# Conditioning vectors of two adaLN layers: one layer in pairs of chunks on TensorE, the other summed on VectorE, and a token-major mLSTM output

## The chip, the cores and the metric

One core of one Trainium2 chip. The metric is the device time of one execution in microseconds (us), smaller is better. Engines: PE (TensorE), DVE (VectorE), ACT (ScalarE), POOL (GpSimd), SP (the queue that issues nearly all loads).

## The reference, cut to what matters

```python
def hybrid_layer(xl, xc, c, c_ctx, w_ada, b_ada, ...):
    mod_l = (jax.nn.silu(c) @ w_ada + b_ada)[:, None, :]
    mod_c = jax.nn.silu(c_ctx) @ w_ada + b_ada
    sh1_l, sc1_l, g1_l, sh2_l, sc2_l, g2_l = jnp.split(mod_l, 6, -1)
    ...
    hl = rms_norm(xl, norm_mix) * (1.0 + sc1_l) + sh1_l
    hc = rms_norm(xc, norm_mix) * (1.0 + sc1_c) + sh1_c
    ...                      # attention, bidirectional mLSTM, pooling
    xl = xl + g1_l * (jnp.concatenate([att_l, ml_l, pool_l], -1) @ w_out)
    h2l = rms_norm(xl, norm_ffn) * (1.0 + sc2_l) + sh2_l
    xl = xl + g2_l * swiglu(h2l, w_ffn_gate, w_ffn_up, w_ffn_down)
    ...                      # the same for the context xc, in layer 0 alone
```

All in float32: model width 1024, 256 latent and 256 context tokens, two such layers, then a second block of another kind that the change does not touch. `w_ada` is 1024 x 6144 per layer (24 MB): six parts of 1024 columns (0 `sh1`, 1 `sc1`, 2 `g1`, 3 `sh2`, 4 `sc2`, 5 `g2`), multiplied with two vectors, `c` and `c_ctx`. Layer 1 leaves the context's output out, so of its parts 2 to 5 only the vector `c` is needed.

## The kernel before, in words

**Order of the work.** Layer 0: prologue (normalization, first three projections), mixer (17 projections of `w_in`, mLSTM, attention, pooling), `w_out` with the next norm ("norm0"), a FFN in two halves of 11 tiles, "norm1". Layer 1: the same for the 256 latent tokens, then the second block. Inside the mixer, generators of projections, mLSTM, attention, pooling, `w_out` and conditioning are drawn in turn by `_mix` with the numbers of the table `MIX` (line 24); a scheduler then sets the order on each engine.

**Weights.** Every dense product runs as three products of split operands (`mm3`, lines 234 to 238). `weights` (line 223) loads a tile of 512 KB into a ring of four (`wr`, by SP, line 220), ACT copies it to `wh` (line 229) and DVE makes the rest `wl` (line 230); `wh` has three buffers, `wl` two. A load into a slot of `wr` waits until what was in the slot has been read.

**Conditioning** (`ada`, lines 364 to 395). A layer's 6144 columns are 24 chunks of 256. Per chunk: two tiles of 512 KB into the same ring `wr`, eight matmuls in which the vectors, padded to 32 columns (`cs`), are stationary and the weights move (line 375; four groups of 32 PSUM rows hold partial sums over k), an ACT copy to `ade` (line 384), two transpositions (line 387), and on DVE a sum over the four groups, the bias and for two of the parts a third operation (lines 389 to 393). Layer 0 takes 8 chunks in the prologue and 16 in its mixer; layer 1 takes 10 in the mixer of layer 0, 2 each in norm0 and norm1, and 10 in its own mixer.

```python
            for k0 in (0, 4):
                _, v = self.raw(w, k0, 4, 256 * ch, 256)
                for g in range(4):
                    nc.tensor.matmul(bank[32 * g:32 * g + 32, 0:256], self.cs[:, k0 + g, :], v[:, g, :],
                                     start=k0 == 0, stop=k0 == 4)
```

**FFN of layer 0.** `ffn_up` (gate, silu, up, product at line 733, split at line 258) and `resid` (down) draw one dense product after another. No conditioning runs here before the change.

**mLSTM.** `hs` holds the outputs as [token, head, tile, 64]; at the end it is scaled by its inverse norm, and each pair of heads of a tile is gathered to `hc` by DVE (line 967) and transposed (line 968). The stabilizer M goes to DRAM (`Md`) through SP.

Of the kernel before, what the change touches and what calls it, by code (L numbers as in the profile page):

```python
# [23 lines left out]
MIX = {0: {'order': 'k0 g q0 v1 v0 a2 k1 q1 av a1 a0 a3 ak o0 p0 o1 p1', 'ada_own': 16, 'ada_next': 10, 'proj': 2, 'ml': 5, 'att': 1, 'fill': 1, 'late': 3, 'ada': 1, 'split': 0, 'split2': 1}, 1: {'order': 'ak k0 g a0 v0 q0 a1 av k1 q1 v1 a2 a3 p0 o0 o1 p1', 'ada_own': 10, 'ada_next': 0, 'proj': 3, 'ml': 9, 'att': 2, 'fill': 1, 'late': 1, 'ada': 1}, 2: {'in': 4, 'att': 2, 'solve': 1, 'att2': 5, 'gate': 1, 'even': 1, 'odd': 1, 'fill': 9, 'early': 5}, 'ada_ffn': [0, 0], 'norm0': 2, 'norm1': 2}  # L24
# [128 lines left out]
def _run(g):  # L153
    for _ in g:
        pass


class Builder:
    def __init__(self, tc, ctx, a):
# [10 lines left out]
        self.reg, self.reg_ins, self.reg_use = None, None, []  # L170
        self.rooms = []
# [42 lines left out]
    def raw(self, w, k0, nk, c0, cw, t=None):  # L214
# [5 lines left out]
        self.last = self.nc.sync.dma_start(v, ap).ins.name  # L220
# [130 lines left out]
    def norm_first(self, x, rr, segs, xh, xl):  # L351

        nc = self.nc
        for k in range(8):
            xr, t = (self.wk.tile([128, self.wt], F32, name=n) for n in ("sq", "nt"))
            (nc.gpsimd if k % 3 == 2 else nc.vector).tensor_mul(xr, x[:, k], rr)
            for s, e, A, B in segs:
                nc.scalar.activation(xh[:, k, s:e], xr[:, s:e], AF.Identity, bias=B(k), scale=A(k))
                nc.vector.tensor_scalar(t[:, s:e], xr[:, s:e], A(k), B(k), op0=OP.mult, op1=OP.add)
            nc.vector.tensor_sub(xl[:, k], t, xh[:, k].bitcast(F32))  # L360
            yield


    def ada(self, l, n, ahead=0, at=(3,)):
# [5 lines left out]
        def products(i, ch):  # L370
            bank = self.ps(at[i % len(at)], [128, 512])
            for k0 in (0, 4):
                _, v = self.raw(w, k0, 4, 256 * ch, 256)
                for g in range(4):
                    nc.tensor.matmul(bank[32 * g:32 * g + 32, 0:256], self.cs[:, k0 + g, :], v[:, g, :],  # L375
                                     start=k0 == 0, stop=k0 == 4)
            return bank

        banks = []
        for i, ch in enumerate(todo):  # L380
            banks += [products(j, todo[j]) for j in range(len(banks), min(n, i + ahead + 1))]
# [4 lines left out]
            for i in range(2):  # L386
                nc.tensor.transpose(pt[:, i, :], e[:, 128 * i:128 * i + 128], self.ident)
            m = mod[:, 2 * ch:2 * ch + 2, :]
            nc.vector.tensor_reduce(m, pt.rearrange("p n (g j) -> p n j g", g=4)[:, :, 0:2, :], axis=AX.X, op=OP.add)
            nc.vector.tensor_add(m, m, vec[f"b_ada{l}"][:, 2 * ch:2 * ch + 2, None].to_broadcast([128, 2, 2]))  # L390
            if ch // 4 in (1, 4):
                nm, k = vec[f"norm_mix{l}" if ch // 4 == 1 else f"norm_ffn{l}"], 2 * (ch % 4)
                nc.vector.scalar_tensor_tensor(m, m, 1.0, nm[:, k:k + 2, None].to_broadcast([128, 2, 2]),
# [4 lines left out]
    def first(self):  # L398
        nc, a, tc = self.nc, self.a, self.tc
        x = self.x = self.xp.tile([128, 8, 512], F32, name="x")  # L400
        with ExitStack() as es:
# [11 lines left out]

            add, _, r = self.squares(512)
# [11 lines left out]
            self.ada_todo = [[4, 0, 5, 1, 6, 2, 7, 3] + list(range(8, 24)) for _ in range(2)]  # L426
            pre = self.layer(0, r, self.ada(0, 8, 1, (1,)), None)
# [12 lines left out]
    def layer(self, l, pre, beside, done):  # L440
# [8 lines left out]
        with ExitStack() as es:  # L449
            ap = es.enter_context(tc.tile_pool(name=f"mix{l}", bufs=1, reuse_waits="tile"))  # L450
            if both:
                xh, xl = self.normed()
                norm = self.norm_first(x, pre, [(0, 256, m(1, 1), m(0, 1)), (256, 512, m(1, 0), m(0, 0))], xh, xl)
# [1200 lines left out]
```

## Time and profile before

| | |
|---|---|
| median of 3 runs | 1876.68 us (1875.64 to 1877.19) |
| the profiled execution, its own time | 1877.25 us |
| its span in the profile | 1875.5 us |
| PE busy | 1805.5 us, 96% |
| DVE / ACT / POOL busy | 59% / 49% / 14% |
| bytes moved | 279.32 MB, mean 149 GB/s |

"Busy" is the share of the span in which the engine executes. A chain that ended last names at each step what released it. Windows give, for a stretch of the span, the busy time of each engine (and its count of instruction records), the granted clock of PE as a share of 2.4 GHz, the share of the DMA engines in use, and what they moved. One matmul of `ada` leaves two records.

The stages that the change touches, by their bounds in the span: prologue 0 to 58 us, layer 0's mixer 58 to 300 (projections until about 193.6, then attention, mLSTM and pooling), norm0 300 to 340, layer 0's FFN 340 to 700, norm1 700 to 735, layer 1's mixer 735 to 890.

### The profile page before, as it was taken

To read this page: it belongs to the slowest core of one execution; us is meant where nothing else is said; L and a number is where in the kernel's file an instruction comes from. 1 tells how busy PE (TensorE), PEld (TensorE's weight loads), DVE (VectorE), ACT (ScalarE), POOL (GpSimd) and SP (SyncE) were. 2 spreads that over 40 slices of the span, in tenths; PEclk is the share of its full clock that TensorE was granted. 3 is DMA by queue.
4 is the path that set the end of the run, shared out by engine and by line. 5 is a ranking of instruction groups with operands and counts; after the bars stand their busy time and mean duration, and the time that the engine had idled before them with its cause. 6 is when DMAs were issued, how large, how long until landed. Compare 5 with 4: busy or idle time off the path is not lost.

```text
span 1875.5 us, 34091 instructions
## 1 busy us (share of the span) xinstructions
PE 1805.5 (96%) x13552; PEld 1593.1 (85%) x13552; DVE 1112.7 (59%) x2122; ACT 918.4 (49%) x1654; POOL 261.6 (14%) x357
## 2 busy tenths in 40 slices
PE   7999999999999999999999999998999999899998
PEld 4677567888888897877999999998999988799998
DVE  4566656433333365786676655667878864466654
ACT  4455467322222365656554644446676544454443
POOL 1011423000000021231000210012565010010000
PEclk8999999999999999999999999999999999999999
DMA  9443567432333265345666656666554540166664
GB/s 295 131 129 91 180 202 234 126 91 77 103 104 99 75 180 169 111 141 178 183 185 197 191 171 182 182 194 169 158 140 124 136 128 11 39 177 179 184 184 127
DMA packets 490608, 279.32 MB, mean 149 GB/s; under 512 B 18241, under 2 KB 487241, under 8 KB 490321
## 3 DMA queue, kind: packets, MB, share of 16 engines
q1 hardware_dynamic: 490016, 275.33, 50.5%
q8 instruction: 106, 1.74, 0.4%
q10 hardware_dynamic: 432, 1.82, 0.3%
q14 instruction: 54, 0.43, 0.1%
HBM read 274.99 MB, written 2.12 MB: 148 GB/s over the span
## 4 chain that ended last, share of the span: by engine, by line
PE 83%; DVE 5%; DMA 5%; ACT 3%; issue 3%; POOL 1%; SPq 0%; ACTq 0%; POOLq 0%; DVEq 0%
PE pd L236 17%; PE pd L238 17%; PE pd L237 17%; PE p L236 6%; PE p L237 6%; PE p L238 6%; PE p L375 2%; DMA wr<-in_w_in_dram 1%; DVE wl L230 1%; DMA wr<-in_w_ada_dram 1%; PE p L808 1%; PE p L789 1%; PE p L1498 1%; ACT wh L229 1%; PE p L940 1%
## 5 line engine op out<-in xcount | busy, mean ns | idle before, releaser
L229 ACT ACTIVATE wh<-wr 128x1024 fp32r<-128x1024 f32 (+4 forms) x450 | 436.6, 972 | 628.5 <-PE pd L237 311.1
L230 DVE TENSOR_TENSOR wl<-wr,wh 128x1024 fp32r<-128x1024 f32 (+4 forms) x450 | 509.7, 1134 | 176.8 <-PE pd L238 98.7
L236 PE MATMUL pd<-xh,wh 128*128 128x256 f32 (+1 forms) x1168 | 362.8, 312 | 13.5 <-ACT wh L229 7.4
L238 PE MATMUL pd<-xh,wl 128*128 128x256 f32 (+1 forms) x1168 | 358.0, 307 | 1.5 <-DVE wl L230 1.3
L236 PEld LDWEIGHTS pd<-xh,wh 128*128 128x128 f32 x1168 | 224.6, 193 | 31.1 <-ACT wh L229 9.1
L238 PEld LDWEIGHTS pd<-xh,wl 128*128 128x128 f32 x1168 | 224.9, 193 | 15.7 <-DVE wl L230 5.6
L236 PE MATMUL pd<-hh,wh 128*128 128x256 f32 (+1 forms) x781 | 228.3, 294 | 0.0
L237 PE MATMUL pd<-hl,wh 128*128 128x256 f32 (+1 forms) x781 | 227.4, 293 | 0.0
L237 PE MATMUL pd<-xh,wh 128*128 128x256 f32 x792 | 225.8, 285 | 0.0
L238 PE MATMUL pd<-hh,wl 128*128 128x256 f32 (+1 forms) x781 | 223.5, 294 | 0.2 <-DVE wl L230 0.2
L315 POOL TENSOR_TENSOR ssa<-ssa,sq 128x256 f32<-128x256 f32 x54 | 49.4, 915 | 796.2 <-ACT sq L313 525.6
L237 PEld LDWEIGHTS pd<-xh,wh 128*128 128x128 f32 x792 | 152.3, 192 | 1.6 <-issue 1.2
L236 PEld LDWEIGHTS pd<-hh,wh 128*128 128x128 f32 x781 | 146.8, 188 | 4.8
L237 PEld LDWEIGHTS pd<-hl,wh 128*128 128x128 f32 x781 | 146.7, 188 | 4.6
L238 PEld LDWEIGHTS pd<-hh,wl 128*128 128x128 f32 x781 | 144.8, 188 | 4.9 <-DVE wl L230 0.4
L237 PE MATMUL pd<-xl,wh 128*128 128x512 f32 (+1 forms) x376 | 132.4, 354 | 0.0
L733 DVE TENSOR_TENSOR sg<-sg,p 128x256 f32<-128x256 f32 (+1 forms) x66 | 33.6, 510 | 158.4 <-PE p L238 158.1
L236 PE MATMUL p<-xh,wh 128*128 128x256 f32 (+1 forms) x360 | 103.1, 286 | 0.0
L238 PE MATMUL p<-xh,wl 128*128 128x256 f32 x352 | 99.8, 283 | 0.0
L237 PE MATMUL p<-xh,wh 128*128 128x256 f32 x352 | 99.8, 283 | 0.0
L237 PEld LDWEIGHTS pd<-xl,wh 128*128 128x128 f32 x376 | 72.9, 194 | 11.2 <-issue 1.5
L687 DVE SCALAR_TENSOR_TENSOR x<-pd,mod,x 128x256 f32<-128x256 f32 x88 | 40.9, 480 | 67.2 <-PE pd L238 67.2
(471 smaller groups left out, 3871.8 us busy)
## 6 DMA issues: line engine op xcount, KB each, us to landing
wr<-in_w_ada_dram SPq DMA_DIRECT2D x96, 512.0 KB, 4.4
wr<-in_w_in_dram SPq DMA_DIRECT2D x92, 512.0 KB, 3.8
wr<-in_w_ffn_gate_dram SPq DMA_DIRECT2D x44, 512.0 KB, 3.7
wr<-in_w_ffn_up_dram SPq DMA_DIRECT2D x44, 512.0 KB, 3.8
wr<-in_ffn_w_gate_dram SPq DMA_DIRECT2D x44, 512.0 KB, 3.8
wr<-in_ffn_w_up_dram SPq DMA_DIRECT2D x44, 512.0 KB, 3.8
wr<-in_ffn_w_down_dram SPq DMA_DIRECT2D x32, 448.0 KB, 3.7
wr<-in_w_out_dram SPq DMA_DIRECT2D x40, 256.0 KB, 3.1
```

The lines of the kernel that those rows point to most:

```text
L229: nc.scalar.activation(h[:, :n], t[:, :n], AF.Copy)
L230: nc.vector.tensor_sub(l[:, :n], t[:, :n], h[:, :n].bitcast(F32))
L236: mm(ps, wh, xh, start=start, stop=False)
L237: mm(ps, wh, xl, start=False, stop=False)
L238: mm(ps, wl, xh, start=False, stop=stop)
L315: eng.tensor_add(acc, acc, sq)
L375: nc.tensor.matmul(bank[32 * g:32 * g + 32, 0:256], self.cs[:, k0 + g, :], v[:, g, :], start=k0 == 0, stop=k0 == 4)
L687: nc.vector.scalar_tensor_tensor(x[:, n, s:s + 256], ps[:, s - c0:s - c0 + 256], g(n), x[:, n, s:s + 256], op0=OP.mult, op1=OP.add)
L733: nc.vector.tensor_mul(g, g, ps)
L789: nc.tensor.matmul(s, qq[:, e, 128 * qt:128 * qt + 128], kk[:, kv, i, 0:128 * nk], start=i == 0, stop=i == 1)
L808: nc.tensor.matmul(po[64 * e:64 * e + 64, :], avt[:, kt, 64 * kv:64 * kv + 64], pts[e][:, kt, :], start=kt == 0, stop=kt == nk - 1)
L940: nc.tensor.matmul(po[:, t - lo, :], wt[d][s][t], mvt[:, s, h, :], start=i == 0, stop=i == len(use) - 1)
```

## The change

Four parts.

1. `ada` serves layer 0 but for part 5, and the last two pairs of layer 1, in **pairs** of chunks: 16 matmuls into one bank, one ACT copy, two transpositions, two DVE additions (a third operation for some parts). A pair loads four tiles of 512 KB. Four pairs stand in the prologue (with a ring `wa` of seven tiles of their own), six in layer 0's mixer (in the ring `wr`), one each in norm0 and norm1 (layer 1, chunks 20 to 23, part 5).
2. `ada_sums`, new: part 5 of layer 0 and parts 0 to 4 of layer 1, in twelve halves of 512 columns, **on DVE during layer 0's FFN**. A half takes eight tiles of 128 x 512 (256 KB, a ring `ar` of four, by SP), each multiplied by the vector's element and accumulated (`av`); for six halves with both vectors, for six with `c` alone. PE then sums over the partitions with a stationary `sums` of 32 columns (8 or 4 matmuls of 128 columns), ACT copies, PE transposes once, DVE adds the bias. Two steps are drawn after each dense product of the FFN.
3. In the prologue x times its inverse norm is computed before the conditioning (`xr`), and `gate` keeps the SP loads of further `w_in` weights behind the last conditioning load.
4. In the mLSTM `hs` becomes [token, tile, head, 64], is scaled head by head, and the transpositions read it directly; the 12 copies `hc` are gone. `Md` is written by ACT's queue.

```diff
-MIX = {0: {..., 'ada_own': 16, 'ada_next': 10, ...}, 1: {..., 'ada_own': 10, 'ada_next': 0, ...}, ..., 'ada_ffn': [0, 0], 'norm0': 2, 'norm1': 2}
+MIX = {0: {..., 'ada_own': 6, ...}, 1: {...}, ..., 'norm0': 1, 'norm1': 1}
...
-        self.last = self.nc.sync.dma_start(v, ap).ins.name
+        d = self.nc.sync.dma_start(v, ap).ins
+        if self.gate:
+            self.tc.add_manual_dep(d, self.gate, NOSYNC, reason="what comes first goes first")
+        self.last = d.name
...
-        def products(i, ch):
+        def products(i, c, step):
             bank = self.ps(at[i % len(at)], [128, 512])
...
+            for k0 in range(0, 8, 4):
+                if step == 1:
+                    ts = [self.raw(w, k0 + k, 2, 256 * c, 512, new_raw())[1] for k in (0, 2)]
+                    v = lambda k, j: ts[k // 2][:, k % 2, 256 * j:256 * j + 256]
+                else:
+                    ts = [self.raw(w, k0, 4, 256 * (c + j), 256, new_raw())[1] for j in (0, step)]
+                    v = lambda k, j: ts[j][:, k, :]
+                for k in range(4):
+                    for j in range(2):
+                        g = 2 * (k % 2) + j
+                        nc.tensor.matmul(bank[32 * g:32 * g + 32, 0:256], self.cs[:, k0 + k, :], v(k, j),
+                                         start=k0 + k < 2, stop=k0 + k > 5)
...
+            nc.vector.tensor_add(m, pv[:, 0, :, :, 0:2], two(wide(vec[f"b_ada{l}"])))
+            nc.vector.tensor_add(m, m, pv[:, 1, :, :, 0:2])
...
+    def ada_sums(self, todo):
+        steps = [(t, k) for t in todo for k in range(8)]
...
+                t = self.sgp.tile([128, 512], F32, name="ar", bufs=4)
+                nc.sync.dma_start(t, self.a["w_ada"][l][128 * k:128 * k + 128, 1024 * p + 512 * h:1024 * p + 512 * h + 512])
...
+        for i, ((l, p, h, js), k) in enumerate(steps):
+            load(i + 3)
...
+            for j, v in zip(js, vs):
+                c = self.cs[:, k, j:j + 1]
+                if k:
+                    nc.vector.scalar_tensor_tensor(v, t, c, v, op0=OP.mult, op1=OP.add)
+                else:
+                    nc.vector.tensor_scalar(v, t, c, None, op0=OP.mult)
+            if k < 7:
+                yield
+                continue
+            bank = self.ps(1, [128, 256])
+            for j, v in enumerate(vs):
+                for g in range(4):
+                    nc.tensor.matmul(bank[32 * g:32 * g + 32, 0:128], self.sums[:, j], v[:, 128 * g:128 * g + 128],
+                                     start=j == 0, stop=j == n - 1)
+            e = self.wk.tile([128, 256], F32, name="ade")[:, 0:128]
+            nc.scalar.activation(e, bank[:, 0:128], AF.Copy)
+            nc.tensor.transpose(bank[:, 128:256], e, self.ident)
...
-            self.ada_todo = [[4, 0, 5, 1, 6, 2, 7, 3] + list(range(8, 24)) for _ in range(2)]
-            pre = self.layer(0, r, self.ada(0, 8, 1, (1,)), None)
+            self.ada_todo = [(k, 4) for k in range(4)] + [(c, 1) for c in range(8, 20, 2)], [(20, 1), (22, 1)]
+            xr = self.room("xr", [128, 8, 512])
+            for k in range(8):
+                (nc.gpsimd if k % 3 == 2 else nc.vector).tensor_mul(xr[:, k], x[:, k], r)
+            pre = self.layer(0, xr, self.ada(0, 4, 1, (1,), self.ring("wa", [128, 1024], 7)), None)
...
+                    if k == 6:
+                        self.gate = self.last
...
-                ada = _chain(self.ada(l, n["ada_own"], at=(2,)), self.ada(1, n["ada_next"], at=(2,)))
+                ada = self.ada(l, n["ada_own"], at=(2,)) if both else iter(())
...
-                _run(_mix((up, 4), (self.ada(1, MIX["ada_ffn"][f] if both else 0, 1, (1,)), 1)))
+                if both and f == 0:
+                    ahead = self.ada_sums([(0, 5, h, (0, 1)) for h in range(2)] +
+                                          [(1, p, h, (0, 1)) for p in (1, 0) for h in range(2)] +
+                                          [(1, p, h, (0,)) for p in (2, 4, 3) for h in range(2)])
+                _run(_until(up, 1, (ahead, 2)) if both else up)
...
-            nc.sync.dma_start(self.Md[d, :, 0:T], M[32 * d:32 * d + 4, T0:])
+            nc.scalar.dma_start(self.Md[d, :, 0:T], M[32 * d:32 * d + 4, T0:])
...
-        hs = ap.tile([128, 4, ntt, 64], F32, name="hs")
+        hs = ap.tile([128, ntt, 4, 64], F32, name="hs")
...
-                hc = ap.tile([128, 2, 64], F32, name="hc", bufs=1)
-                nc.vector.tensor_copy(hc, hs[:, 2 * tl:2 * tl + 2, t, :])
-                nc.tensor.transpose(ps[:, t, :], hc.rearrange("p a b -> p (a b)"), self.ident)
+                nc.tensor.transpose(ps[:, t, :], hs[:, t, 2 * tl:2 * tl + 2, :].rearrange("p a b -> p (a b)"), self.ident)
```

How the order on the engines moves, at three places.

PE, in layer 0's mixer between projections, before: one chunk (line 375) with its transpositions (line 387) among the mLSTM's products (lines 908 and 940) and the last matmul of a projection.

```order
L238 MATMUL pd<-xh,wl 128x512
L375 MATMUL p_1186<-wr,cs 32x256 x8
L908 MATMUL p_1174<-qs,ks 128x256 x2
L908 MATMUL p_1300<-qs,ks 128x256 x2
L513 MATMUL p_1288<-sq,cm 128x512
L387 MATMUL p_1186<-cm,ade 128x128 x2
```

The same kind of place in the changed kernel (its line 387 is the matmul of `ada`, 399 the transposition, 1000 and 1032 the mLSTM's products, 240 to 242 those of `mm3`).

```order
L1032 MATMUL p_776<-mvt,W_767 128x65
L387 MATMUL p_794<-wr,cs 32x256 x16
L1000 MATMUL p_931<-qs,ks 128x512 x2
L1000 MATMUL p_945<-qs,ks 128x512 x2
L240 MATMUL pd<-xh,wh 128x512
L241 MATMUL pd<-xl,wh 128x512
L399 MATMUL p_794<-cm,ade 128x128 x2
```

A pair's 16 matmuls stand together, after the 5th, 7th, 9th, 11th, 13th and 15th of the 17 projections, and the next projection follows with little between.

PE, late in layer 0's mixer, in the attention's scores, transpositions and products (lines 789, 802, 808), before: a chunk every second step.

```order
L375 MATMUL p_2156<-wr,cs 32x256 x8
L789 MATMUL p_2453<-kk,qq 128x256 x2
L802 MATMUL p_2358<-cm,pr 128x128 x4
L789 MATMUL p_2488<-kk,qq 128x256 x2
L387 MATMUL p_2156<-cm,ade 128x128 x2
L808 MATMUL p_2238<-pt,avt 64x256 x7
L802 MATMUL p_2430<-cm,pr 128x128 x2
L375 MATMUL p_2189<-wr,cs 32x256 x8
```

There in the changed kernel (lines 881, 894, 900).

```order
L894 MATMUL p_2268<-cm,pr 128x128 x4
L881 MATMUL p_2324<-kk,qq 128x256 x2
L894 MATMUL p_2285<-cm,pr 128x128 x4
L900 MATMUL p_2240<-pt,avt 64x256
L881 MATMUL p_2338<-kk,qq 128x256 x2
L894 MATMUL p_2301<-cm,pr 128x128 x4
```

The attention's steps follow one another with no conditioning between them.

DVE, in layer 0's FFN, before: the split of weights (line 230), the product of gate and up (733) and its split (258).

```order
L733 TENSOR_TENSOR sg<-sg,p_3563 128x512
L230 TENSOR_TENSOR wl<-wr,wh 128x1024
L258 TENSOR_TENSOR hl<-sg,hh 128x512
L230 TENSOR_TENSOR wl<-wr,wh 128x1024
```

There in the changed kernel (825, 234 and 262 are those three lines, 441 and 443 the accumulation of `ada_sums`).

```order
L825 TENSOR_TENSOR sg<-sg,p_3244 128x512
L234 TENSOR_TENSOR wl<-wr,wh 128x1024
L262 TENSOR_TENSOR hl<-sg,hh 128x512
L443 TENSOR_SCALAR av_3334<-ar,cs 128x512
L443 TENSOR_SCALAR av_3335<-ar,cs 128x512
L441 SCALAR_TENSOR_TENSOR av_3334<-ar,cs,av_3334 128x512
L441 SCALAR_TENSOR_TENSOR av_3335<-ar,cs,av_3335 128x512
L234 TENSOR_TENSOR wl<-wr,wh 128x1024
```

Four accumulations stand between two weight splits, one split per dense product. On PE the sums over partitions come as 72 matmuls in 18 separate places among the FFN's products.

## Rows read from the trace of the kernel before

**Rows 1.** The page: busy time by engine, and the chain that ended last.

```profile
PE 1805.5 (96%) x13552; PEld 1593.1 (85%) x13552; DVE 1112.7 (59%) x2122; ACT 918.4 (49%) x1654; POOL 261.6 (14%) x357
...
PE 83%; DVE 5%; DMA 5%; ACT 3%; issue 3%; POOL 1%; SPq 0%; ACTq 0%; POOLq 0%; DVEq 0%
```

**Rows 2.** Windows by stage: bounds, length, busy per engine, clock, DMA share, GB/s.

```profile
0.00:58.00 58.00, 45.68 (x258) 26.84 (x258) 28.29 (x72) 24.16 (x43) 5.93 (x9) 0.88 0.84 267
58.00:193.60 135.60, 126.82 (x700) 99.32 (x700) 84.44 (x202) 67.49 (x140) 16.99 (x17) 0.97 0.37 109
193.60:300.00 106.40, 99.83 (x759) 61.11 (x752) 60.18 (x204) 61.26 (x152) 32.16 (x50) 1.00 0.69 218
340.00:700.00 360.00, 358.99 (x1764) 298.87 (x1763) 132.94 (x172) 114.49 (x163) 8.98 (x12) 1.00 0.35 102
735.00:890.00 155.00, 149.13 (x1071) 122.12 (x1069) 115.11 (x293) 96.80 (x207) 36.48 (x43) 0.98 0.48 141
```

**Rows 3.** The same windows, line 375 alone (PE, PEld).

```profile
58.00:193.60 135.60, 6.79 (x96) 2.61 (x96) 0.97 0.37 109
193.60:300.00 106.40, 23.09 (x328) 8.47 (x320) 1.00 0.69 218
735.00:890.00 155.00, 10.95 (x144) 4.05 (x144) 0.98 0.48 141
```

**Rows 4.** The same windows, line 387 alone (the transpositions).

```profile
193.60:300.00 106.40, 8.17 (x42) 5.20 (x42) 1.00 0.69 218
```

**Rows 5.** Prologue: PE's timeline (start, length, what), last conditioning product.

```profile
46.76 1.07 PE L375 MATMUL p<-wr,cs 128*32 128x256 f32 x16
```

**Rows 6.** Prologue: a window between loads.

```profile
30.00:35.00 5.00, 5.00 (x40) 2.79 (x39) 0.50 (x3) 0.47 (x2) 0.00 (x0) 1.00 0.49 161
```

**Rows 7.** PE's timeline around one chunk in a dense stretch.

```profile
169.97 0.40 PE L237 MATMUL pd<-xl,wh 128*128 128x512 f32 x1
170.20 0.39 PE L238 MATMUL pd<-xh,wl 128*128 128x512 f32 x1
170.52 1.07 PE L375 MATMUL p<-wr,cs 128*32 128x256 f32 x16
171.52 0.50 PE L236 MATMUL pd<-xh,wh 128*128 128x512 f32 x1
171.86 0.39 PE L237 MATMUL pd<-xl,wh 128*128 128x512 f32 x1
```

**Rows 8.** SP's timeline, two stretches of weight loads.

```profile
171.22 0.99 SPq L220 DMA_DIRECT2D wr<-in_w_in_dram  x2
...
294.19 15.58 SPq L220 DMA_DIRECT2D wr<-in_w_out_dram  x13
```

**Rows 9.** The page, DMA issues: count, KB each, us to landing.

```profile
wr<-in_w_in_dram SPq DMA_DIRECT2D x92, 512.0 KB, 3.8
```

**Rows 10.** ACT's timeline: the copy of those weights and its wait.

```profile
176.36 1.06 ACT L229 ACTIVATE wh<-wr 128x1024 fp32r<-128x1024 f32 x1 [2.54 <-DMA wr<-in_w_in_dram]
```

**Rows 11.** Windows in layer 0's mixer (columns as in rows 2).

```profile
150.00:160.00 10.00, 8.37 (x33) 7.31 (x34) 8.11 (x19) 5.86 (x11) 0.00 (x0) 0.66 0.63 193
170.00:180.00 10.00, 7.33 (x56) 5.57 (x54) 5.63 (x14) 4.18 (x8) 3.11 (x5) 1.00 0.41 110
266.69:282.88 16.19, 15.63 (x137) 9.29 (x136) 8.98 (x40) 12.14 (x34) 4.69 (x8) 1.00 0.82 265
```

**Rows 12.** ACT's groups by form in 266.69 to 282.88.

```profile
L384 ACT ACTIVATE ade<-p 128x256 f32<-128x256 f32 x4 | 1.5, 386 | 2.0 <-PE p L375 1.9
```

**Rows 13.** DVE's groups by form, whole span: count, busy us, mean ns.

```profile
L230 DVE TENSOR_TENSOR wl<-wr,wh 128x1024 fp32r<-128x1024 f32 x308 | 380.5, 1236 | 123.6 <-PE pd L238 79.7 <-issue 21.0 <-ACT wh L229 16.7
...
L733 DVE TENSOR_TENSOR sg<-sg,p 128x512 f32<-128x512 f32 x22 | 15.1, 687 | 102.0 <-PE p L238 102.0
...
L731 DVE SCALAR_TENSOR_TENSOR sg<-sg,sb 128x256 f32<-128x256 f32 x22 | 10.5, 478 | 0.0
...
L263 DVE SCALAR_TENSOR_TENSOR raw<-x,mod,raw 128x256 fp32r<-128x256 f32 x8 | 5.4, 672 | 0.1
```

More of the change, by code (lines that the diff above doesn't have):

```diff
@@ L170, in __init__ @@
         self.reg, self.reg_ins, self.reg_use = None, None, []
+        self.gate = None
         self.rooms = []
@@ L368, in ada @@
         todo = [self.ada_todo[l].pop(0) for _ in range(n)]
-        def products(i, ch):
+        def products(i, c, step):
             bank = self.ps(at[i % len(at)], [128, 512])
[L372 to L376, printed above, removed]
+            new_raw = lambda: new() if new else None
+            for k0 in range(0, 8, 4):
[10 more added lines that the diff above has]
+                                         start=k0 + k < 2, stop=k0 + k > 5)
             return bank
         banks = []
-        for i, ch in enumerate(todo):
-            banks += [products(j, todo[j]) for j in range(len(banks), min(n, i + ahead + 1))]
+        for i, (c, step) in enumerate(todo):
+            banks += [products(j, *todo[j]) for j in range(len(banks), min(n, i + ahead + 1))]
             bank = banks[i]
@@ L385, in ada @@
             pt = bank[:, 256:512].rearrange("p (i q) -> p i q", i=2)
[L386 to L393, printed above, removed]
+            for j in range(2):
+                nc.tensor.transpose(pt[:, j, :], e[:, 128 * j:128 * j + 128], self.ident)
@@ L412, in first @@
                 self.fn(cs[:, :, j], vec[n], AF.Silu)
+            self.sums = cst.tile([128, 2, 32], F32, name="sums")
+            nc.gpsimd.memset(self.sums, 0.0)
+            for j in range(2):
+                nc.gpsimd.memset(self.sums[:, j, j:j + 1], 1.0)
             add, _, r = self.squares(512)
@@ L573, in layer @@
                 for k in range(0, 8, 2):
-                    next(beside)
-                    if k < 6:
+                    if k:
                         next(beside)
+                    if k == 6:
+                        self.gate = self.last
                     if k:
@@ L581, in layer @@
                 products(6)
-                for _ in range(2):
+                for _ in range(4):
                     self.close_room()
@@ L595, in projections @@
                         self.late_consts()
+                        self.gate = None
             if both:
@@ L663, in layer @@
                     self.columns2()
-                _run(self.resid(rows, hs, ks, T0, 512, m(5, 1), m(5, 0), None if both else done))
+                res = self.resid(rows, hs, ks, T0, 512, m(5, 1), m(5, 0), None if both else done)
+                _run(_until(res, 1, (ahead, 2)) if both else res)
     def normed(self):
```

61 lines of the change are left out of this document (48 added, 13 removed).

## Prediction, written before the changed kernel ran

> **What bounds the kernel now.** I read the busy times and the chain first [rows 1]: TensorE is busy for 96% of the span and makes 83% of the chain, no other engine reaches 60%. So time is saved only where PE executes less or waits less, and lost where work is laid on PE or another engine is pushed past PE's pace. Next the windows by stage [rows 2]. What matters there is length minus PE's busy time: the projections of layer 0 (58 to 193.6 us) hold 8.8 us of waits, the rest of that mixer (193.6 to 300) 6.6, layer 1's mixer 5.9, layer 0's FFN only 1.0. DVE has 227 us free of 360 in that FFN, and the DMA moves 102 GB/s there against 218 in the attention. The change moves work from places where everything is busy to the place with the most room; the question is what PE pays for it.
>
> **Price of a chunk.** Conditioning alone [rows 3] shows 16 records per chunk: 6 chunks among the projections, 20.5 in the rest of the mixer, 9 in layer 1's. In the dense stretch [rows 7] matmuls start 0.23 us apart. From 170.20 to 171.86 two such spacings (0.46) should pass, and 1.66 do: the chunk costs 1.20, namely 1.00 of its own and 0.09 going in and 0.11 coming out. A transposition is 8.17/42 = 0.195 us [rows 4]. A chunk is 1.20 + 0.39 = 1.59 us of PE; a pair, with one switch and two transpositions, 2.00 + 0.20 + 0.39 = 2.59.
>
> **The change, part by part.**
>
> *Prologue: -5 us (-2 to -10).* The bytes are the same: 8 chunks. Their loads no longer stop: from 30 to 35 us the DMA was at half share and 161 GB/s [rows 6], against 267 over the prologue [rows 2], because each chunk waited for a slot of the ring; the own ring of seven and the `gate` keep conditioning in front. The last conditioning product, at 46.76 [rows 5], could come some 9 us earlier, but then normalization and first products must follow; I take half. Upper bound -10 (all of it), lower -2 (norm and `w_in` behind the gate are late instead). One copy less per pair and x*r ahead of time lie beside the loads: nothing.
>
> *Projections of layer 0: +15 (+8 to +25).* Six pairs cost 15.5 against 9.5 for six chunks: +6. Then the wait. A pair takes all four slots of `wr`, so the next two projections' weights start loading only when its matmuls have begun: for one chunk, that began at 170.52, the loads were issued 0.70 later [rows 7, 8]; landing takes 3.8 us in the median [rows 9] (here ACT began 5.14 after the issue [rows 10]), the copy 1.06. So the next projection starts about 0.7 + 3.9 + 1.06 + 0.2 = 5.9 us after the pair, and PE has its 2.2 and some 0.7 of mLSTM products meanwhile: 3.0 of wait for five pairs, half of that for the last, 16.6 in all. The 8.8 of waits before are of the same kind and go: +8. Bounds: landing at 3.8 with twice the cover gives half of it, 5.14 in place of 3.9 adds 7. For the clock +1: 0.66 in 150 to 160 (full and half speed mixed, two thirds of the time at 1.2 GHz), where PE is idle for 1.6 of 10 us, but 1.00 in 170 to 180 with 2.7 idle [rows 11]. So waits of this size do not by themselves bring half speed.
>
> *Rest of layer 0's mixer: -27 (-19 to -34).* 20.5 chunks leave PE, 20.5 x 1.59 = 32.6 us. Not all comes back: in an eight-step stretch of attention (16.19 us) PE is busy 15.63, of which four chunks are 6.4, and ACT 12.14, of which the four copies `ade` are 1.5 [rows 11, 12]. Without them ACT needs 10.6 and PE 9.3: ACT and its chain with DVE become the bound, and I take 12.5 to 14 per eight steps, not 10.6. On the other hand the last chunks hold up the loads of `w_out` on SP, which stream only from 294.19 [rows 8]; those are now loaded ahead: some 6 us of waits. -34 is chunks and waits without loss, -19 attention at 14.5.
>
> *norm0 and norm1: -1.* One pair for two chunks, 2.59 for 3.18, twice.
>
> *FFN of layer 0: +11 (+8 to +15).* The new PE work stands in the open, since PE is full here [rows 2]. 72 matmuls of 128 columns: eight of 256 took 1.00 [rows 7], so by columns 72 x 0.0625 = 4.5, by count 9.0; 5 taken, as they are of the same four groups. 18 places with 0.20 of switching: 3.6. Twelve transpositions: 2.3. ACT's twelve copies and the additions are hidden. On DVE a half with two vectors adds 16 operations of 128 x 512 to 4 splits (1.236), 2 products (0.687) and 2 splits of 128 x 512 (taken the same) [rows 13]. Of the form used there is only a 128 x 256, 0.478; from 512 to 1024 columns an operation grows by 0.549, so 256 more give 0.478 + 0.27 = 0.75 us (bounds: 0.687, a plain product of that size, and 2 x 0.672, the slowest row of that form). That makes 12.0 + 7.7 = 19.7 us in the 96 matmuls of four projections, 22.1: 89%, it fits. A half with `c` alone needs 13.7. The extra 25 MB raise the DMA here from 102 to about 172 GB/s, well under what it moves elsewhere [rows 2]. SP's loads of `ar` wait for DVE, and weights queue behind them, but the weights run four tiles ahead.
>
> Here the Trainium skill speaks against the change: TensorEngine Tiling (Array Packing), section Tiling Modes (Key Properties), says that changing the tiling mode drains TensorE, and sums with 32 stationary columns change it twice at each place. The trace agrees, 0.09 and 0.11 us [rows 7]; without it the FFN's term would be 7.3, with it 10.9.
>
> *Layer 1's mixer: -13 (-7 to -17).* Ten chunks of 1.59 = 15.9 leave it. PE waits more there once it is lighter (ACT is busy 96.8 and DVE 115 of 155 [rows 2]); 3 given back, at worst half.
>
> *mLSTM.* Twelve small copies on DVE before the transpositions, and a queue for `Md`, at the mixers' ends: within the two mixers' terms, nothing of its own (0 to -1).
>
> The sum: -5 + 15 - 27 - 1 + 11 - 13 = -20, from the profiled 1877.25 to 1857.2; the median of the runs lies 0.57 below it, so **1857 us**.
>
> **Rivals.**
>
> *A: the clock pays for the pairs.* Each of the six waits after a pair costs a stretch like that of 150 to 160: 10 us at 0.66, 3.4 us each [rows 11], 20 in place of 1. Then 1876, no change. For it: a pair's wait is longer than a chunk's. Against it: 170 to 180, at full clock with more idle time; and the whole of 58 to 193.6 has 0.97 [rows 2], which is 4 us lost over all its waits. Chance 0.12. The Trainium skill, TensorE: Matmul & The Clock Gate (HAM oscillation), describes just this: waits for DMA between short stretches of products send the array back to half speed. One window here agrees (0.66), another with more idle time does not (1.00).
>
> *B: slower; DVE becomes the bound in the FFN.* With 16 accumulations in 22.1 us less 7.7, it decides at 0.90 us each. At 1.2 the half takes 4.8 us too long, at 1.34 (twice 0.672 [rows 13]) 7.1; six halves with two vectors make 28 to 42, so 1885 to 1899. For it: the slow rows of that form, and an accumulation that reads its own last result. Against it: the 0.478 row, and POOL's 9 us in 360, while it is busier elsewhere [rows 2]. Chance 0.10.
>
> *C: better.* The waits after pairs are filled (the order leaves mLSTM and attention beside them): +5 in place of +15; attention runs at the pace of ACT's busy time, -34; layer 1 gives back nothing, -17. Then 1836. For it: PE follows at once wherever data is there (FFN: 1.0 us of waits). Against it: attention's chain runs through four engines, and weights after a pair cannot have been loaded. Chance 0.16.
>
> That the change does not do what it says is out: the order shows the pairs, the sums and an attention without conditioning.
>
> **How the numbers follow.** The forecast has 0.62, with a range of its own of 1844 to 1870: the terms' half-ranges of 4, 8.5, 7.5, 3.5 and 5, added as independent ones, make 13. A, B and C have 0.12, 0.10 and 0.16. About 0.2%, 3.8 us, is what a measurement of this kernel can tell from no change. Faster: forecast, C and a little of A, 0.80; same: most of A, 0.08; slower: B and the upper edge of A, 0.12. The range 1836 to 1879 leaves out B, half of C and the upper edge of A: 0.2.
>
> **What would show it.** Prologue: no conditioning product after some 40 us. Projections: six waits of about 3 us of `pd` for `wh`, each behind a pair, and the stretch about 15 longer. Attention: eight steps in 12.5 to 14 us, waits for ACT. FFN: about 371 us, DVE near 60% over it and near 90% in its first half, accumulations of 0.75 us. Layer 1's mixer about 142. The forecast is wrong if the accumulations exceed 0.9 us, if the clock falls below 0.9 over the projections, or if the attention does not quicken.

## The result, and the profile after

The change makes the kernel slower: 1904.39 us median of 5 runs (1900.22 to 1908.63) against 1875.64 for the kernel before in the same job, ratio 1.0151, 95% interval 1.0135 to 1.0167. The prediction was 1857 us, with a range of 1836 to 1879. The profiled execution is the slowest of the five runs, 1908.63, with a span of 1906.8, so the stages below differ by 31.3 us in sum where the medians differ by 28.75.

The page of the changed kernel, answering to [rows 1] (busy time by engine, then the chain):

```profile
PE 1806.2 (95%) x13252; PEld 1593.5 (84%) x13252; DVE 1192.3 (63%) x2200; ACT 908.7 (48%) x1630; POOL 262.5 (14%) x366
...
PE 84%; DVE 5%; ACT 3%; DMA 3%; issue 2%; POOL 1%; SPq 0%; POOLq 0%; ACTq 0%; DVEq 0%
```

PE is as busy as before, 1806.2 us against 1805.5, although conditioning takes less of it. To see where the time lies, both executions are cut at the same pieces of work: the last product of the first three projections, the last copy of a projection of layer 0, the first FFN product of layer 0, its last gate or up product, the first FFN product of layer 1. Before (bounds, length, busy time by engine, clock, DMA share, GB/s):

```profile
0.00:57.10 57.10, 45.26 (x257) 26.79 (x257) 27.73 (x71) 23.26 (x41) 5.93 (x9) 0.88 0.85 271
57.10:194.50 137.40, 128.14 (x706) 99.96 (x705) 85.19 (x203) 68.78 (x143) 17.65 (x17) 0.98 0.37 108
194.50:330.80 136.30, 128.13 (x990) 86.41 (x987) 84.45 (x256) 86.15 (x209) 45.53 (x65) 0.99 0.70 219
330.80:643.50 312.70, 311.59 (x1370) 253.16 (x1370) 105.87 (x133) 87.50 (x114) 1.70 (x2) 0.99 0.32 95
643.50:889.50 246.00, 236.18 (x1749) 202.56 (x1748) 167.72 (x381) 147.66 (x299) 50.86 (x63) 0.98 0.52 152
```

And after:

```profile
0.00:57.70 57.70, 47.05 (x249) 27.59 (x249) 27.02 (x63) 21.63 (x37) 5.89 (x12) 0.85 0.85 268
57.70:246.00 188.30, 156.63 (x828) 115.64 (x826) 91.86 (x227) 74.25 (x155) 20.52 (x22) 0.86 0.37 114
246.00:361.70 115.70, 100.16 (x600) 73.78 (x598) 66.84 (x182) 74.18 (x177) 41.23 (x63) 0.94 0.24 72
361.70:686.60 324.90, 323.79 (x1525) 256.07 (x1526) 199.41 (x293) 90.38 (x126) 1.70 (x2) 0.99 0.54 169
686.60:922.60 236.00, 223.45 (x1568) 197.70 (x1568) 164.59 (x357) 142.78 (x288) 51.69 (x66) 0.96 0.41 114
```

| stage | before | after | difference | forecast |
|---|---|---|---|---|
| prologue | 57.1 | 57.7 | +0.6 | -5 |
| projections of layer 0 | 137.4 | 188.3 | **+50.9** | +15 |
| rest of that mixer, norm0 | 136.3 | 115.7 | -20.6 | -27.5 |
| FFN of layer 0, most of it | 312.7 | 324.9 | +12.2 | +11 |
| norm1 and layer 1's mixer | 246.0 | 236.0 | -10.0 | -13.5 |
| all behind | 986.0 | 984.2 | -1.8 | 0 |

(norm0 and norm1 were forecast together at -1; half of it is put to each.) Four of five terms came out within 7 us. The projections alone are 36 us beyond theirs, and that is more than the whole gain hoped for.

**What the 50.9 us are.** PE's idle time there went from 9.3 us (137.4 - 128.14) to 31.7, so 22.4 is waiting. The other 28.5 is busy time, and the pairs explain 6 of it. The granted clock fell from 0.98 to 0.86: in the trace 51.0 us of this stretch lie at half clock (1.2 GHz) and PE is busy in 43.4 of them, against 6.8 before. Work at half clock takes nearly twice as long, as the spacing of matmuls below shows, so the clock cost at most half of the difference, some 18 us. What is left, some 4 us, is work that has moved into the stretch: by the counts of matmuls, 24 of the attention, the pooling and the end of the mLSTM lie in it now that lay behind it before. The waits, by what ended them (PE in 57.7 to 246; total us, times, longest):

```profile
PE pd L240 <- ACT wh L233: 13.4, 9, 3.4
PE p L387 <- ACT nd L1035: 6.3, 4, 2.7
PE p L399 <- ACT ade L396: 4.5, 3, 3.0
```

The first is the wait for weights that the forecast had. The other two it did not have: a pair's first matmul waits until ACT has read the mLSTM's output from the same PSUM bank, and its transpositions wait for the copy `ade`, with little or nothing else between them.

One pair, on PE's timeline (start, length, what, in brackets the idle time before):

```profile
224.76 1.93 PE L387 MATMUL p<-wr,cs 128*32 128x256 f32 x32
227.19 0.44 PE L399 MATMUL p<-cm,ade 128*128 128x128 f32 x2 [0.50 <-ACT ade L396]
231.02 0.79 PE L240 MATMUL pd<-xh,wh 128*128 128x512 f32 x1 [3.39 <-ACT wh L233]
...
234.18 0.63 PE L240 MATMUL pd<-xh,wh 128*128 128x512 f32 x1
234.60 0.63 PE L241 MATMUL pd<-xl,wh 128*128 128x512 f32 x1
235.03 0.63 PE L242 MATMUL pd<-xh,wl 128*128 128x512 f32 x1
...
236.22 0.39 PE L242 MATMUL pd<-xh,wl 128*128 128x512 f32 x1
236.45 0.39 PE L240 MATMUL pd<-xh,wh 128*128 128x512 f32 x1
236.68 0.39 PE L241 MATMUL pd<-xl,wh 128*128 128x512 f32 x1
```

From the pair's start to the next projection 6.3 us pass, and over the six pairs 5.9 to 9.0; the forecast worked out 5.9. What it missed stands behind the wait: matmuls follow one another at 0.42 us, until near 236, and only then at the 0.23 of [rows 7]. That is half clock, and it follows every pair: in the trace's record of the clock it begins 4.5 to 9.2 us after the start of each of the six. Three windows of 8 us show one turn of it; 0.58 is mostly 1.2 GHz, and 1.00 is 2.4:

```profile
170.00:178.00 8.00, 5.53 (x15) 4.18 (x14) 4.99 (x10) 2.94 (x4) 0.00 (x0) 0.58 0.73 247
178.00:186.00 8.00, 8.00 (x35) 6.48 (x35) 0.00 (x0) 1.18 (x2) 0.00 (x0) 1.00 0.00 1
186.00:194.00 8.00, 7.79 (x58) 6.92 (x56) 5.24 (x18) 4.90 (x11) 2.48 (x2) 1.00 0.00 0
```

The DMA column shows where the wait for weights comes from. It runs at 247 GB/s, then stands still for 16 us, and then all is wanted at once. SP's queue has the same turn:

```profile
195.52 0.99 SPq L221 DMA_DIRECT2D wr<-in_w_in_dram  x2
196.61 10.03 SPq L221 DMA_DIRECT2D wr<-in_w_ada_dram  x4
225.46 1.72 SPq L221 DMA_DIRECT2D wr<-in_w_in_dram  x2
```

The weights of two projections, four tiles of conditioning, and then nothing until 225.46, because all four slots of the ring hold tiles for a pair that PE reaches at 224.76.

### The profile page after: what moved, and what is told of

The parts are those of the page before. It is cut to its first block, busy times and chain, and to the rows that moved or that the text cites. A ratio compares the mean times of both kernels' runs of the same rounds, so it can differ in the third digit from the quotient of the medians.

```text
span 1906.8 us, 33662 instructions
## 1 busy us (share of the span) xinstructions
PE 1806.2 (95%) x13252; PEld 1593.5 (84%) x13252; DVE 1192.3 (63%) x2200; ACT 908.7 (48%) x1630; POOL 262.5 (14%) x366
## 4 chain that ended last, share of the span: by engine, by line
PE 84%; DVE 5%; ACT 3%; DMA 3%; issue 2%; POOL 1%; SPq 0%; POOLq 0%; ACTq 0%; DVEq 0%
PE pd L240 18%; PE pd L242 18%; PE pd L241 18%; PE p L242 6%; PE p L240 6%; PE p L241 6%; DMA wr<-in_w_in_dram 2%; PE p L900 1%; PE p L1032 1%; PE p L387 1%; DVE wl L234 1%; PE p L1588 1%; PE p L894 1%; ACT wh L233 1%; PE p L881 1%
## 5 line engine op out<-in xcount | busy, mean ns | idle before, releaser
L241 PE MATMUL pd<-xl,wh 128*128 128x512 f32 (+1 forms) x376 | 137.3, 367 | 0.0
L441 DVE SCALAR_TENSOR_TENSOR av<-ar,cs,av 128x512 f32<-128x512 f32 x126 | 89.8, 747 | 10.2 <-DMA ar<-in_w_ada_dram 9.4
```

Source lines behind the costliest of these rows:

```text
L241: mm(ps, wh, xl, start=False, stop=False)
L441: nc.vector.scalar_tensor_tensor(v, t, c, v, op0=OP.mult, op1=OP.add)
```

## The experiments

All are the changed kernel with one edit, unless another is named. Ratios are to the kernel before, run on the same chip.

### The pairs without their loads

The matmuls stay and multiply a constant. The conditioning of parts 2 to 4 of layer 0 is not computed.

```diff
             for k0 in range(0, 8, 4):
-                if step == 1:
+                if still:
+                    v = lambda k, j: self.cm[:, 0:256]
+                elif step == 1:
...
-                ada = self.ada(l, n["ada_own"], at=(2,)) if both else iter(())
+                ada = self.ada(l, n["ada_own"], at=(2,), still=True) if both else iter(())
```

> The changed kernel, but the six pairs of layer 0's mixer multiply a constant that already lies in SBUF instead of weights: their 24 loads of 512 KB are left out (so the conditioning of parts 2 to 4 of layer 0 is not computed), their 96 matmuls, copies and transpositions stay. Theory (ring): a pair's four tiles fill the whole ring of weights, the next projection's weights load only afterwards, PE idles and its clock falls; without the loads the projections (57.9 to 246 us, 188 us) fall to about 143 to 148, PE's idle time there from 31.7 to some 8 to 10, the granted clock from 0.86 to 0.96 or more, the whole to 1860 to 1866 us. Rival 1 (pairs themselves): the 32-column matmuls, the transposition's wait for the copy and the bank shared with the mLSTM cause it; then only the 13.4 us of waits for weights go, the clock stays under 0.9 and the whole is 1888 to 1892. Rival 2 (order): the mLSTM's new order causes it; then nothing changes, 1902 to 1906.

Measured: 1867.30 us, ratio 0.9948 (0.9926 to 0.9970). The projections take 139.0 us, idle time is 6.9 and the clock 0.91. Cut at 158 us:

```profile
55.90:158.00 102.10, 101.58 (x556) 78.87 (x555) 62.38 (x124) 53.39 (x103) 16.36 (x15) 1.00 0.31 83
158.00:194.90 36.90, 30.52 (x176) 23.79 (x176) 23.58 (x74) 15.21 (x41) 4.16 (x4) 0.68 0.03 8
```

Up to 158 us, with three of the pairs in it, PE idles for 0.5 us and the clock is full. So 32-column matmuls do not by themselves bring the clock down, and with the loads 49 of the 50.9 us are gone: both rivals, at 1888 us or more for the whole, are out. One thing is not separated. Without the loads the scheduler also set the pairs further apart, after some 7, 11 and 14 of the 17 projections and two more at 16, so the waits for the bank and for the copy may have gone with the distance. Three details differ from what was expected. The stretch fell below 143, partly because one pair now stands after the projections; the clock is 0.91 instead of 0.96, all of it lost in the last 37 us, where PE idles for 6.4 us again, on the mLSTM (3.1 for `qs`) and once on the bank at a pair (2.1); and the whole is 1.3 us above the 1866 expected.

### PE kept busy in the waits

```diff
+            if busy:
+                d = self.ps(1, [128, 512])
+                for _ in range(busy):
+                    f = nc.tensor.matmul(d[:, :384], self.ident, self.cm[:, :384], start=True, stop=True)
+                    self.tc.add_manual_dep(f.ins, m.ins.name, NOSYNC, reason="behind the pair")
             return bank
...
-                ada = self.ada(l, n["ada_own"], at=(2,)) if both else iter(())
+                ada = self.ada(l, n["ada_own"], at=(2,), busy=6) if both else iter(())
```

> The changed kernel with six matmuls of 128 x 384 on a constant added behind each of the mixer's six pairs; their result is not used. They do nothing but keep PE occupied while it waits for weights. At full clock they take 3.8 us per pair, about what a pair's wait for weights takes, 23 us in all if none of it lay in the waits. Theory (clock): the projections lose as much by half clock as by idling (23 us each), and the clock falls because PE idles; then the granted clock over the projections rises from 0.86 to 0.95 or more, and the whole falls by 12 to 20 us, to 1884 to 1892, though PE has more to do. Rival 1 (idling alone counts, or the clock falls for another reason, such as the 32-column matmuls): clock stays at 0.86 to 0.88, whole 1904 to 1925. Rival 2 (the matmuls delay the chain behind them): clock up, but no gain, 1900 to 1910.

Measured: 1901.65 us, ratio 1.0124 (1.0097 to 1.0150). In the projections (57.2 to 234.5 us, to set beside 57.70:246.00 above):

```profile
57.20:234.50 177.30, 164.00 (x877) 118.85 (x876) 87.41 (x212) 70.09 (x144) 19.17 (x19) 0.93 0.39 121
```

Some 23.5 us of matmuls of no use were added, and the stretch became 11.0 us shorter. Idle time fell by 18.4 (31.7 to 13.3), so 5 us of the added work were a cost, and by this sum the clock gave back about 16; by PE's busy time at half clock, which fell from 43.4 to 19.0 us, it gave back 12. Within the stretch the theory has the direction right. For the whole it does not: the gain is hardly 3 us, under the 12 expected, with intervals that overlap those of the changed kernel, and 1901.65 with a clock that rose is the case of rival 2. Part of the difference shows: the clock came to 0.93, not 0.95, with other waits that stay (5.9 us for the bank at the pairs), and 4.0 of the 11.0 us were lost again in the rest of the mixer (119.7 for 115.7). What is shown: with PE's idle time filled, the granted clock of the stretch rises. That idling alone brings it down is not shown; the pairs in four steps, below, have a stretch that speaks against it.

### The pairs in two steps: the version to use

```diff
+            if halves:
+                bank = products(i, c, step, (0,))
+                yield
+                products(i, c, step, (4,), bank)
+            else:
...
-                ada = self.ada(l, n["ada_own"], at=(2,)) if both else iter(())
+                ada = self.ada(l, n["ada_own"], at=(2,), halves=True) if both else iter(())
```

(`products` takes the halves of k and the bank as arguments.)

> The changed kernel, but a pair of the mixer comes in two steps: the first two tiles with their eight matmuls, and in the next round the other two. SP then loads two projections' weights between them, so the ring never holds four conditioning tiles. Some pairs move behind the projections. Theory (ring): the projections' stretch falls from 188 to about 145 to 155, clock to 0.95 or more, but three pairs now lie in the attention (2.6 us each, partly beside its waits): whole 1862 to 1876 us. Rival 1 (pairs themselves): as many pairs in sum, 1895 to 1905. Rival 2 (loads of any kind in front of the weights): little changes, 1890 to 1905.

Measured: 1868.44 us, ratio 0.9944 (0.9914 to 0.9975). It computes all that the reference asks for, and is faster than both kernels, by 0.56% against the kernel before. Projections, then the rest of the mixer with norm0:

```profile
57.70:197.30 139.60, 130.82 (x716) 102.15 (x718) 88.24 (x213) 69.95 (x146) 21.83 (x21) 0.96 0.39 114
197.30:317.80 120.50, 106.38 (x715) 74.74 (x709) 71.34 (x195) 77.92 (x185) 43.26 (x64) 0.99 0.38 115
```

260.1 us in sum, against 304.0 with whole pairs and 273.7 before. The wait of `pd` for `wh` is down to 4.3 us over the whole mixer. By the medians, which come from different jobs, the gain over whole pairs is 36 us; the 44 compare the slowest execution of one kernel with one of the quicker ones of the other.

Two things changed at once. SP loads the weights of two projections between the halves of a pair, as meant; and as each half takes a turn, a pair comes after every fourth projection and not after every second, so that three of the six came to stand behind the projections. The traces speak for the second. PE executes the second and the third pair all but in one piece, and before the third the ring does hold four tiles of conditioning, those issued at 123.89 and at 142.95, so that the next weights are issued only at 171.10:

```profile
123.89 4.72 SPq L221 DMA_DIRECT2D wr<-in_w_ada_dram  x2
131.97 3.70 SPq L221 DMA_DIRECT2D wr<-in_w_in_dram  x2
142.95 9.05 SPq L221 DMA_DIRECT2D wr<-in_w_ada_dram  x2
171.10 2.08 SPq L221 DMA_DIRECT2D wr<-in_w_in_dram  x2
```

Behind the third pair, which starts at 170.40, other work of PE covers this; behind the second, which starts at 122.09, the old wait is there in full:

```profile
130.74 0.80 PE L240 MATMUL pd<-xh,wh 128*128 128x512 f32 x1 [3.80 <-ACT wh L233]
```

Whole pairs after every fourth projection were not run, so what the splitting is worth by itself is open.

### The pairs in four steps, most of them in the attention

```diff
+            if parts:
+                bank = self.ps(at[i % len(at)], [128, 512])
+                for k0 in range(0, 8, 2):
+                    v = self.raw(w, k0, 2, 256 * c, 512)[1]
...
+                    if k0 < 6:
+                        yield
+            else:
```

> The changed kernel with a pair in four steps of one tile and four matmuls each: SP loads two projections' weights between any two of them, so conditioning holds one or two of the ring's four slots, and only seven of 24 tiles lie among the projections, the others in the attention behind them. Theory (ring, and PE has room in the attention): projections 130 to 136 us at a clock of 0.97 or more, the rest of the mixer 122 to 132, mixer 255 to 264 in all (changed kernel: 304), whole 1859 to 1870 us. Rival (pairs among the attention cost their full price and hold up its chain): rest of the mixer 135 or more, whole 1873 to 1885.

Measured: 1872.81 us, ratio 0.9982 (0.9956 to 1.0008), no change that can be told.

```profile
58.00:186.10 128.10, 124.91 (x628) 97.39 (x627) 81.04 (x188) 66.86 (x138) 20.57 (x19) 0.93 0.38 105
186.10:328.00 141.90, 122.57 (x802) 84.48 (x799) 80.79 (x220) 80.59 (x194) 44.46 (x66) 0.95 0.38 117
```

The projections are the shortest of all, 11.5 us under those with pairs in two steps, but the rest is 21.4 us longer, with four of the six pairs in it instead of three: 270.0 us in sum against 260.1. The rival held: the rest takes 141.9 us, over its 135, and the whole lies a hair under its 1873. PE idled there for 14.1 of 120.5 us with three pairs and idles for 19.3 of 141.9 with four; the idle time of the attention is no room in which a pair is hidden. Some of its tiles are late as well (4.5 us of waits for `w_ada` there).

The clock of the projections, expected at 0.97 or more, is 0.93, although PE idles for only 3.2 of their 128.1 us. All of it was lost in one place:

```profile
162.30:179.30 17.00, 15.78 (x80) 12.13 (x80) 15.50 (x50) 10.97 (x29) 1.01 (x1) 0.50 0.07 14
```

PE had idled for 1.1 us just before and did so once more in it (1.1). What it executed there were the mLSTM's products, those of 65 columns above all, and one pair; no dense product of a projection. So half clock can last for 17 us with PE busy in 93% of them, and what PE executes may count as well as its idling. No run separates the two.

### Without the sums in the FFN

The twelve halves are constants here; nothing of `ada_sums` is executed.

```diff
+            nc.gpsimd.memset(self.mod[0][:, 40:48], 0.5)
+            nc.gpsimd.memset(self.mod[1][:, 0:40], 0.5)
...
-                _run(_until(up, 1, (ahead, 2)) if both else up)
+                _run(up)
```

> The changed kernel without the sums on VectorE in layer 0's FFN: part 5 of layer 0 and parts 0 to 4 of layer 1 are constants, their loads, accumulations, matmuls, copies and transpositions are left out. If the sums cost PE only its own matmuls, switches and transpositions, the FFN is 11 to 12 us shorter and the whole 1891 to 1894. If they also delay the weights or slow the clock elsewhere (layer 1's mixer, norm1), more than 15 us shorter, under 1889. If they hide, under 4 us, over 1900.

Measured: 1905.01 us (1899.28 to 1911.05), ratio 1.0150 (1.0088 to 1.0213), no faster than with the sums and outside the 1891 to 1894 expected. Yet its FFN is as short as expected, 312.3 us for 324.9. The first row is that FFN, the second all from layer 1's last gate and up product to the end:

```profile
358.80:671.10 312.30, 311.48 (x1369) 252.98 (x1370) 106.29 (x133) 87.60 (x114) 1.70 (x2) 0.99 0.33 95
1044.30:1898.60 854.30, 823.48 (x7350) 790.67 (x7348) 546.55 (x895) 434.94 (x753) 139.82 (x199) 0.98 0.52 147
```

That last stretch takes 845.5 us in the changed kernel, with the same 7350 records on PE. A second kernel without the sums was to tell whether this was chance: the one with pairs in two steps, with the same constants.

> The kernel with pairs in two steps, and without the sums on VectorE in layer 0's FFN: part 5 of layer 0 and parts 0 to 4 of layer 1 are the same constants as in the run without sums. It tells whether the second block, which no edit touches, is slower with these constants (854 us there against 845 to 850 in the other runs, from the first block's last product on). If the constants do it: FFN 12 to 13 us shorter than with sums, second block 852 us or more, whole 1862 to 1870. If it was chance of that run: second block 845 to 850, whole 1853 to 1858.

Measured: 1863.56 us, ratio 0.9929 (0.9907 to 0.9951), and the last stretch again at 853.6:

```profile
1007.20:1860.80 853.60, 822.32 (x7350) 790.53 (x7348) 545.91 (x895) 434.80 (x753) 136.92 (x199) 0.98 0.52 148
```

So it was no chance, and the whole came to 1863.6 as the first case said; the FFN is 313.6 us for 325.0, a little less gain than the 12 expected. But the expectation had put constants against chance, and a third cause appeared: in both kernels without sums the scheduler set PE's instructions in the second block in another order than in the kernels with them, though no line there was edited. The traces say where it matters. The kernel before takes 847.1 us for this stretch; PE's order here differs from it at 12 of some 7300 places, all between 507 and 515 us from the start of the stretch, and there 6.1 of the 6.5 us are lost. The same eight matmuls, first in the changed kernel and then here:

```profile
1564.77 0.66 PE L1622 MATMUL p<-G,XP 128*64 128x128 f32 x8 [1.83 <-ACT XP L1618]
1514.66 1.12 PE L1624 MATMUL p<-G,XP 128*64 128x128 f32 x8 [4.22 <-ACT XP L1620]
1515.10:1525.00 9.90, 9.90 (x112) 8.53 (x108) 2.31 (x8) 2.48 (x7) 1.15 (x4) 0.51 0.18 55
```

A wait 2.4 us longer than in the changed kernel, and some 10 us at half clock behind it (last line), make up the loss. So the loss goes with the order at one place; no run has that order without the constants. For the sums themselves the stage is the measure: 11.4 to 12.6 us of the FFN.

### The mLSTM's part alone

The kernel before with part 4 of the change, as in its diff.

> The kernel before with the mLSTM's part of the change alone: outputs token by token, scaled head by head, transpositions straight from them, the stabilizer written by ACT's queue. Theory: 1873 to 1877, no change or up to 3 us faster. Rival: the order moves and the mLSTM becomes later, so that part of the loss in the projections is here: 1880 to 1900.

Measured: 1876.55 us, ratio 1.0005 (0.9982 to 1.0028). It is worth nothing by itself and does no harm.

### The prologue with four loads fewer

```diff
-                if step == 1:
+                if new and c > 1 and k0 == 4:
+                    pass
+                elif step == 1:
```

> The changed kernel, but the last two of the prologue's four pairs use their first two tiles twice: four loads of 512 KB are left out, so the conditioning of parts 0 and 1 of layer 0 is partly another one; instructions of the engines stay the same. If the prologue is bound by the bytes it loads (2 MB at 267 GB/s is 7.9 us), it ends 5 to 8 us earlier, at 50 to 53 us instead of 57.7. If PE's order, the copies or the normalization bound it, it ends within 2 us of 57.7.

(`v` keeps the tiles of the first half, so the kernel leaves out part of the conditioning of layer 0.) Measured in one profiled execution: the prologue ends at 55.6 us, 2.1 earlier than in the changed kernel, with the DMA share down from 0.85 to 0.75. That lies between the two cases, far nearer to the second: the bytes left out, 7.9 us' worth, are not its bound. Even the 2.1 us are uncertain: in the other runs the same prologue, with all its loads, ended between 55.8 us (pairs in two steps without the sums) and 58.0. The chain of waits of the kernel before has, among its long pieces (start, length):

```profile
18.62 5.05 DMA wr<-in_w_ada_dram
...
34.41 5.43 DMA wr<-in_w_ada_dram
```

These are gone in the changed kernel (PE's waits for conditioning tiles in the first 58 us fell from 7.9 to 1.9 us), and in their place stand

```profile
23.42 3.49 DVE xr L503 x4
27.42 2.08 ACT xh L361 x4
```

The multiplications of x that now run ahead, and the first normalized tile, for which PE waits 3.4 us. The last conditioning product, which the forecast had at some 40 us, is no earlier than the 46.76 of [rows 5]:

```profile
47.33 1.06 PE L387 MATMUL p<-wa,cs 128*32 128x256 f32 x14
```

## Why the prediction was wrong

**The step that failed** is the term of the projections, "+15 (+8 to +25)". Its first part, +6 for the pairs, stands. Its second, +8 for the waits, measured +22.4. The single wait for weights was worked out well (5.9 us from pair to projection, 6.3 measured in the row above, though its sum takes 3.9 us for a landing where its row has 3.8), but it was taken as PE's only one. The bank shared with the mLSTM (6.3 us) and the copy `ade` (4.5) were in no term, though the order ahead of the prediction shows that hardly anything stands between a pair's matmuls and its transpositions. Taking the 8.8 us of old waits as replaced by the new ones was the second error: most of them had nothing to do with weights, only 4.3 us of them were.

**The clock was the larger miss**: +1 forecast, some +18 measured; its sign of being wrong, a clock under 0.9 over the projections, came with 0.86. The argument was a row, 170 to 180 us at full clock with 2.7 us of idling [rows 11], against another at 0.66 with 1.6. Two windows of which one says yes and one says no do not carry "waits of this size do not bring half speed"; they say that it depends on more than the length of one wait. Here up to three waits follow one another around a pair, for the bank, the copy and the weights, and half clock came after every pair. Rival A priced this at 20 us and had 0.12. It held in its mechanism and its size; with it alone the forecast would have been 1876. The Trainium skill, TensorE: Matmul & The Clock Gate (HAM oscillation), says that waits for DMA between short stretches of products keep sending the array back to half speed; the trace now agrees, with 0.58 and 1.00 in turn. The run with busy waits shows that idling has a part in it (0.86 to 0.93), the pairs in four steps that it need not be all (17 us at 0.50 with 1.2 us idle).

**The rest of the mixer**, -27 with norm0's half: -20.6, inside its bounds, in part by luck. Neither -27 nor the bounds follow from the forecast's own terms: 32.6 us of chunks and 6 of waits, without loss, make 38.6 and not 34. And some 4 us of the gain are the work that moved ahead into the projections. The forecast had eight steps of attention at 12.5 to 14 us. The same score products of late attention that took 16.9 us before (267.7 to 284.6) stand in the changed kernel in

```profile
303.80:319.30 15.50, 13.12 (x77) 8.26 (x76) 8.65 (x30) 11.60 (x31) 5.42 (x9) 1.00 0.00 1
```

that is 15.5 us, where PE was busy for 15.63 of 16.19 in [rows 11]: no engine is full now, and it hardly quickened. For the eight steps of [rows 11], in the same proportion, that is 14.8 us, outside 12.5 to 14. ACT is busy for 11.6 us, so its busy time is not the bound. That the path of each step, from PE to DVE, ACT and POOL and back, sets the pace is argued, not shown: PE's waits here are short (1.3 us in all for POOL's `pr`, 1.0 for ACT). The larger part of the gain lies before it.

**The FFN**: +11 forecast, +12.2 measured, 12.6 by the run without sums. Rival B, an accumulation over 0.9 us, is out: 0.747 was measured where 0.75 had been worked out from a shape half as wide and the growth per column. DVE was pressed, though less than the 89% worked out for halves with two vectors (in 380 to 480 us it is busy 78 of 100), and PE waited 1.3 us in all for weights there:

```profile
L441 DVE SCALAR_TENSOR_TENSOR av<-ar,cs,av 128x512 f32<-128x512 f32 x126 | 89.8, 747 | 10.2 <-DMA ar<-in_w_ada_dram 9.4
L443 DVE TENSOR_SCALAR av<-ar,cs 128x512 f32<-128x512 f32 x18 | 8.3, 483 | 7.6 <-PE p L451 5.3 <-DMA ar<-in_w_ada_dram 2.2
```

**Layer 1's mixer**: -13 and half of -1 forecast, -10.0 measured. The 3 us of waits given back came out (PE idle 9.8 before, 12.6 after); but PE's busy time fell by 12.7 us where the chunks and norm1's pair were to take off 16.5, and the clock fell from 0.98 to 0.96, for which the sum had no term. **The prologue**: -5 forecast, +0.6 measured. The gap in the loads was real and closed (from 30 to 35 us 312 GB/s where [rows 6] had 161), but SP has issued the 16 conditioning loads only at 40.0 us (38.0 before), and their last product did not come earlier. The work on x that was moved ahead of conditioning joined the path, so "lie beside the loads: nothing" was wrong for it, and the clock was 0.85 instead of 0.88.

**The sign** follows from one resource that the forecast saw and priced too low. With pairs in two steps, and so half as dense among the projections, the mixer and norm0 give -13.6 where the sum had -12.5, and the kernel is 0.56% faster: the plan of the change was right, six whole pairs on a ring of four were not.

## What to carry to other kernels

When a step takes as many slots of a shared ring as the ring has, ask not only how long the next load takes but how often PE will stand still because of it; split the step and set it further apart (here the two came together). Where several short gaps of PE follow one another, put half clock behind them on the list of prices: here the gaps cost 22 us more and the clock some 18. And read a leave-out run by its stages: here a part that costs some 12 us vanished, and the total did not move, because a stage far behind it, which came out in another order, was 8.8 us longer.

## What the runs showed that was not expected

Useless matmuls in the waits made a stretch shorter: 23.5 us of them, and 11.0 us less (clock 0.86 to 0.93), though hardly 3 were left of it in the whole. Half clock lasted from the restart at 231.02 until near 236 before the full rate came back, and in the kernel with pairs in four steps for 17 us with PE busy. In the second block 6 us went with a dozen matmuls in another order: a longer wait, and half clock behind it. And loads of conditioning that no longer stop, 4 of 16 of them even left out, moved the prologue by no more than 2.1 us.
